# Attention values as 64 weight columns, and 16 convolution taps on TensorE, in a two-layer encoder kernel

## The chip, the cores and the metric

The kernel runs on one core of one Trainium2 chip. The metric is device time in microseconds (us): the median of three timed executions is 1800.13 us, the lowest 1799.9, the highest 1801.16. One more execution was recorded by the hardware profiler; all rows below come from it. TensorE is called PE (its weight loads PEld), VectorE DVE, ScalarE ACT, GpSimd POOL, SyncE SP.

## The reference, cut to what matters

Two layers work on x, 512 tokens by 1024 features, float32. Each is a feed-forward block, a mixing block and a second feed-forward block. The change lies in the mixing block alone:

```python
h = rms_norm(x, mix_norm);  p = h @ w_in
# group A: 8 heads, 96 columns for queries and keys, 64 for values, causal in chunks of 64 tokens
probs = softmax(scale * q @ k.T, masked);  attn = probs @ v          # per head, per 128 queries
# group B: 512 channels, causal depthwise convolution of 31 taps
u = a * sigmoid(g)
y[t, c] = conv_b[c] + sum over s in 0..30 of conv_w[30 - s, c] * u[t - s, c]
conv = silu(layer_norm(y, ln_g, ln_b))
x = x + concat(attn, conv) @ w_out
```

## The kernel before, in words

Activations are kept with features on the 128 partitions and the 512 tokens along the free axis. Products with large weights are made of three fp32r matmuls from operands split into a high and a low part (`mm3`, L153 to L157; its three matmuls have lines L154, L155, L156). Attention itself and the transposes are plain fp32 matmuls.

The mixing block is `mix_body` (L617). After the projections of w_in (`conv_in(c)` makes the four convolution groups u[0] to u[3] of 128 channels each, with `glu`), eight heads go through five stages, one step apart each by the table `ORDER = "t0s1p3v4o5"`: `turn` (L808) transposes queries and keys, `scores` (L821) makes scores, mask and exponentials, `turn_p` (L845) transposes the probabilities, `values` (L861) multiplies them with the values, `turn_out` (L879) transposes the result back to features on partitions, and `split` makes its high and low part, one entry of the list `at` for a pair of heads. In `values` the transposed probabilities are the stationary operand (128 columns) and 64 columns of values the moving one: ten matmuls per head, and DVE multiplies the pair's result by the reciprocals of the softmax sums (L875).

Beside the heads runs the convolution, one tap per instruction. The string `CONV = "DAAD"` gives the engine: groups 0 and 3 are accumulated by DVE in a PSUM bank (L922), groups 1 and 2 by ACT, which makes each product (L926), and POOL, which adds it (L930). POOL then sums the four groups (L944 to L946), a matmul with a constant matrix makes the mean over channels (L948), and the layer norm follows: DVE subtracts the mean (L954), squares are summed (L198), the reciprocal root is spread over the partitions (L217), DVE scales (L964), ACT applies silu (L966). Meanwhile PE makes the attention half of the first output products, the early groups (L936 to L940), until the normalised convolution arrives.

The order of instructions on each engine is fixed at build time by a scheduler that weighs estimated times; each engine takes its own list strictly in order. On SP stand the loads of weights; on POOL also the loads that accumulate low parts (L142).

## Time and profile before

| what | value |
|---|---|
| median of three executions | 1800.13 us (1799.9 to 1801.16) |
| the profiled execution, whole | 1798.87 us |
| its span, first to last instruction | 1797.1 us |
| granted PE clock, mean | 1.000 |
| PE busy | 1781.8 us (99%) |
| DVE busy | 1494.5 us (83%) |
| ACT busy | 1107.5 us (62%) |
| POOL busy | 421.5 us (23%) |

In a row of the timeline stand the start in us from the span's first instruction, the duration, engine, line, operation, result and operands, and in brackets how long the engine had been idle and what ended that. A matmul's duration reaches to the end of its way through the array, so that neighbours overlap: the distance from one start to the next is what it costs in a dense row. The profile shows one fp32 matmul as two records ("x2"). Rows of the chain of waits give the time that each piece holds the chain. In the table of windows each engine's busy time within a stretch stands beside the number of its instructions. The attention of the first layer runs from about 449.7 to 506 us, that of the second from 1339.7 to 1395.4 us, and the layer norm of the convolution right behind each.

### The profile page before, as it was taken

The numbers are of one execution on the slowest core, as the hardware profiler recorded it, in microseconds if no ns is written. First come the engines' busy times: TensorE is split into PE (matmuls) and PEld (weight loads), VectorE is DVE, ScalarE is ACT, GpSimd is POOL, SyncE is SP. The second block draws the span as 40 slices with busy tenths as digits, with TensorE's granted clock in tenths as the row PEclk, the third lists the DMA queues.
The fourth block names the chain that finished last, engine by engine and source line by source line (L and its number), as shares of the span: only waits on it lengthen the run. The fifth ranks groups of instructions, "written<-read, shape, count | busy, mean of one in ns | idle before, by whom it ended". The sixth has DMA issues, their size and how long they took to land.

```text
span 1797.1 us, 29235 instructions
## 1 busy us (share of the span) xinstructions
PE 1781.8 (99%) x11334; PEld 1602.4 (89%) x11334; DVE 1494.5 (83%) x2299; ACT 1107.5 (62%) x1721; POOL 421.5 (23%) x343
## 2 busy tenths in 40 slices
PE   9999999999999999999999999999999999999998
PEld 7899999888788899999888999998978788999997
DVE  7898988589956989898779989876998668989883
ACT  5575756457953575756645757554779435756564
POOL 1000000258943000000310000002689410000002
PEclk9999999999999999999999999999999999999999
DMA  5657575325103466665426575743250125575742
GB/s 168 171 131 182 135 177 123 109 88 134 33 22 102 123 164 161 155 160 132 123 65 170 122 194 122 193 112 111 81 147 7 46 82 160 140 183 134 182 117 74
DMA packets 70413, 226.16 MB, mean 126 GB/s; under 512 B 7937, under 2 KB 8321, under 8 KB 70273
## 3 DMA queue, kind: packets, MB, share of 16 engines
q1 hardware_dynamic: 54000, 169.74, 30.3%
q0 software_dynamic: 16128, 54.53, 18.0%
q8 instruction: 89, 1.46, 0.3%
q14 instruction: 52, 0.42, 0.1%
q10 hardware_dynamic: 144, 0.00, 0.0%
HBM read 222.15 MB, written 2.10 MB: 125 GB/s over the span
## 4 chain that ended last, share of the span: by engine, by line
PE 91%; ACT 3%; DVE 2%; POOL 2%; issue 1%; DMA 0%; SPq 0%; ACTq 0%; POOLq 0%; DVEq 0%
PE ps L154 24%; PE ps L156 23%; PE ps L155 23%; PE ps L373 11%; PE ps L374 6%; PE ps L868 1%; PE ps L834 1%; POOL y L930 1%; ACT pr L926 1%; ACT r L840 1%; PE ps L855 1%; PE ps L198 0%; POOL sck L173 0%; PE ps L217 0%; DVE wl L246 0%
## 5 line engine op out<-in xcount | busy, mean ns | idle before, releaser
L155 PE MATMUL ps<-r,wh 128*128 128x256 f32 (+1 forms) x2540 | 806.8, 318 | 0.0
L154 PE MATMUL ps<-r,wh 128*128 128x256 f32 (+1 forms) x2540 | 803.6, 320 | 2.2 <-ACT wh L138 0.7
L156 PE MATMUL ps<-r,wl 128*128 128x256 f32 (+1 forms) x2348 | 749.2, 321 | 0.0
L154 PEld LDWEIGHTS ps<-r,wh 128*128 128x128 f32 x2540 | 480.5, 189 | 47.0 <-ACT wh L138 3.6
L155 PEld LDWEIGHTS ps<-r,wh 128*128 128x128 f32 x2540 | 481.6, 190 | 35.8 <-DVE r L162 1.5
L156 PEld LDWEIGHTS ps<-r,wl 128*128 128x128 f32 x2348 | 445.1, 190 | 33.5 <-DVE wl L144 0.4
L373 PE MATMUL ps<-xj,wh 128*128 128x512 f32 x864 | 303.9, 392 | 0.0
L138 ACT CAST wh<-raw 128x1024 fp32r<-128x1024 f32 (+3 forms) x148 | 131.9, 899 | 208.1 <-PE ps L155 125.8
L390 POOL DMA_DIRECT2D ls<-in_wgu x72 | 62.7, 871 | 734.7 <-ACT ls L389 595.3
L244 ACT CAST wh<-fr 128x1024 fp32r<-128x1024 f32 (+1 forms) x160 | 157.6, 985 | 104.4 <-DVE fr L410 53.2
L144 DVE TENSOR_TENSOR wl<-raw,wh 128x1024 fp32r<-128x1024 f32 (+3 forms) x132 | 145.3, 1108 | 91.3 <-ACT wh L138 90.9
L246 DVE TENSOR_TENSOR wl<-fr,wh 128x1024 fp32r<-128x1024 f32 (+1 forms) x160 | 182.3, 1139 | 20.3 <-ACT wh L244 20.3
L373 PEld LDWEIGHTS ps<-xj,wh 128*128 128x128 f32 x864 | 161.4, 188 | 30.1
L930 POOL TENSOR_TENSOR y<-y,pr 128x511 f32<-128x511 f32 (+14 forms) x120 | 158.6, 1322 | 54.5 <-ACT pr L926 47.1
L374 PE MATMUL ps<-xj,ls 128*128 128x256 f32 x576 | 161.3, 280 | 0.0
L244 ACT CAST wh<-raw 128x1024 fp32r<-128x1024 f32 (+1 forms) x100 | 98.2, 982 | 45.1 <-PE ps L155 24.2
L246 DVE TENSOR_TENSOR wl<-raw,wh 128x1024 fp32r<-128x1024 f32 (+1 forms) x100 | 113.5, 1135 | 14.2 <-ACT wh L244 13.7
L191 POOL TENSOR_TENSOR r<-r,t 128x512 f32<-128x512 f32 x45 | 75.0, 1676 | 175.6 <-ACT t L187 174.8
L374 PEld LDWEIGHTS ps<-xj,ls 128*128 128x128 f32 x576 | 108.3, 188 | 0.0
L389 ACT ACTIVATE ls<-fr 128x1024 fp32r<-128x1024 f32 (+1 forms) x56 | 56.1, 1002 | 74.5 <-PE ps L374 42.8
L926 ACT ACTIVATE pr<-m,vec 128x511 f32<-128x511 f32 (+14 forms) x120 | 85.7, 736 | 13.2 <-POOL y L930 13.2
L922 DVE SCALAR_TENSOR_TENSOR cv<-m,vec,cv 128x511 f32<-128x511 f32 (+14 forms) x120 | 87.8, 732 | 3.6 <-ACT cv L918 2.2
(241 smaller groups left out, 2944.9 us busy)
## 6 DMA issues: line engine op xcount, KB each, us to landing
fr<-in_wgu SPq DMA_DIRECT2D x112, 512.0 KB, 4.2
ls<-in_wgu POOLq DMA_DIRECT2D x72, 512.0 KB, 6.2
raw<-in_wgu SPq DMA_DIRECT2D x62, 512.0 KB, 4.5
fr<-in_wdq SPq DMA_DIRECT2D x48, 384.0 KB, 4.6
ls<-in_wdq POOLq DMA_DIRECT2D x32, 384.0 KB, 4.8
raw<-in_wd SPq DMA_DIRECT2D x32, 384.0 KB, 3.2
raw<-in_wd SPq DMA_DIRECT2D x32, 256.0 KB, 2.8
raw<-in_wcv SPq DMA_DIRECT2D x16, 512.0 KB, 3.6
```

What stands on the lines that cost most here:

```text
L138: order["cast"] = A.copy(hi[:, :w], raw[:, :w]).ins
L144: (G if kind in POOLW.split() else V).tensor_tensor(lo[:, :w], raw[:, :w], hi[:, :w].bitcast(FP), ALU.subtract)
L154: T.matmul(o, lh, rh, start=first, stop=False, skip_group_check=free)
L155: T.matmul(o, lh, rl, start=False, stop=False, skip_group_check=free)
L156: order["mm"] = T.matmul(o, ll, rh, start=False, stop=last, skip_group_check=free).ins
L244: A.copy(hi[:, :w], src[:, :w])
L246: order["lo"] = V.tensor_tensor(lo[:, :w], src[:, :w], hi[:, :w].bitcast(FP), ALU.subtract).ins
L373: T.matmul(o, w[0][:, c], both, start=start and k == 0, stop=False, skip_group_check=True)
L374: last = T.matmul(o[:, 0:HS], w[1][:, c], both[:, 0:HS], start=False, stop=k == 3, skip_group_check=True).ins
L922: V.scalar_tensor_tensor(acc[:, s:], u[c][:, :S - s], tap(k), acc[:, s:], ALU.mult, ALU.add)
L926: A.activation(pr[:, s:], u[c][:, :S - s], AF.Copy, scale=tap(k))
L930: order["conv"] = G.tensor_tensor(acc[:, s:], acc[:, s:], pr[:, s:], ALU.add).ins
```

## The change

1. `values` works on a pair of heads. The values are now the stationary operand (64 columns) and the transposed probabilities the moving one (up to 512 columns); head one of the pair writes partitions 0 to 63 of the result, head two partitions 64 to 127. The result comes out with features on partitions, so `turn_out` has no transposes any more. The reciprocal sums are brought into that layout by eight small matmuls of a broadcast column with the identity (`pr`), copied by ACT, and multiplied in by DVE.
2. The first 16 taps of convolution group 2 are made on PE (`conv_pe`). Sixteen DMAs from SBUF to SBUF put four copies of 32 channels, shifted by 0 to 3 tokens, into each of four tiles; a matmul with a 128 by 32 matrix of tap weights then adds four taps for 32 channels, and four of these per 32 channels, shifted by 0, 4, 8, 12 tokens, make 16 taps. The 15 remaining taps of the group stay with ACT and POOL.
3. The last addition of the sum over groups moves from POOL to DVE. The accumulators of groups 1 and 2 get a buffer each under their own names (before: two buffers under one name), the products four buffers (before three).
4. One early group is placed ahead of the mean's matmul (`E1`), and the output products run in two rounds of four (before three, three, two).

```diff
-CONV = "DAAD"
+TAPS = (0, 31, 31, 0)
+Q = 32
+PT = 16
+PC = 2
+PSTEP = 3
-E1 = 0
-YP = 1
+E1 = 1
-WOG = 3
+WOG = 4
...
+        diag = kpool.tile([P, PT, Q], FP, tag="m", name=nm("m"), bufs=11)
+        G.tensor_tensor(diag, cst[:, None, CI32:CI32 + Q].to_broadcast([P, PT, Q]),
+                        vv(l, "cp")[:, :, None].to_broadcast([P, PT, Q]), ALU.mult)
+        shifted = []
...
-        ys = [None if kind == "D" else kpool.tile([P, S], FP, tag="y", name=nm("y"), bufs=2) for kind in CONV]
+        ys = [kpool.tile([P, S], FP, tag=f"y{c}", name=nm("y"), bufs=1) if n else None for c, n in enumerate(TAPS)]
...
             glu(*pp)
+            if c != PC:
+                return
+            for i in range(4):
+                v = slot()
+                V.memset(v[:, 0:4], 0.0)
+                for r in range(4):
+                    nc.sync.dma_start(out=v[r * Q:(r + 1) * Q, r:], in_=u[c][i * Q:(i + 1) * Q, 0:S - r])
+                shifted.append(v)
+
+        def conv_pe():
+
+            ps = bank()
+            for a in range(PT // 4):
+                for i in range(4):
+                    T.matmul(ps[i * Q:(i + 1) * Q, 4 * a:], diag[:, 4 * a + i], shifted[i][:, 0:S - 4 * a],
+                             start=a == 0, stop=a == PT // 4 - 1)
+            A.activation(ys[PC], ps, AF.Identity, bias=vv(l, "cb")[:, PC:PC + 1])
...
             if h % 2 == 0:
-                heads[h]["po"] = bank()
-            po = heads[h - h % 2]["po"].rearrange("p (t h d) -> p t h d", t=NT, h=2)
-            for t in range(NT):
-                for j in range(t + 1):
-                    T.matmul(po[:, t, h % 2], heads[h]["pt"][j][:, (t - j) * P:(t - j + 1) * P],
-                             vs[j][:, h * DV:(h + 1) * DV], start=j == 0, stop=j == t)
-            if h % 2 == 0:
                 return
             rs = small.tile([P, NT, 2], FP, tag="rs", name=nm("rs"))
             V.reciprocal(rs, heads[h - 1]["sums"])
+            pr = bank()
+            for t in range(NT):
+                for i in range(2):
+                    T.matmul(pr[i * DV:(i + 1) * DV, t * P:(t + 1) * P], rs[:, t, i:i + 1].to_broadcast([P, DV]),
+                             ident, start=True, stop=True)
+            r = tmp()
+            A.copy(r, pr)
+            po = bank()
+            for j in range(NT):
+                for i in range(2):
+                    T.matmul(po[i * DV:(i + 1) * DV, j * P:], vs[j][:, (h - 1 + i) * DV:(h + i) * DV],
+                             heads[h - 1 + i]["pt"][j], start=j == 0, stop=j == NT - 1)
             o = tmp()
-            V.tensor_tensor(o.rearrange("p (t h d) -> p t h d", t=NT, h=2), po,
-                            rs[:, :, :, None].to_broadcast([P, NT, 2, DV]), ALU.mult)
+            V.tensor_tensor(o, po, r, ALU.mult)
             heads[h]["o"] = o
...
-            ps = bank()
-            for t in range(NT):
-                T.transpose(ps[:, t * P:(t + 1) * P], o[:, t * P:(t + 1) * P], ident)
-            at.append(split(ps, kept if len(at) < 2 else slot))
+            at.append(split(heads[h]["o"], kept if len(at) < 1 else slot))
...
         for step in range(H + 6):
+            if step == PSTEP:
+                conv_pe()
...
-                pr = kpool.tile([P, S], FP, tag="pr", name=nm("pr"), bufs=3)
...
+            for s in range(PT if c == PC else 1, n):
+                k = CK - 1 - s
+                pr = kpool.tile([P, S], FP, tag="pr", name=nm("pr"), bufs=4)
+                A.activation(pr[:, s:], u[c][:, :S - s], AF.Copy, scale=tap(k))
...
-        (G if YP else V).tensor_tensor(ysum, ysum, ys[3], ALU.add)
+        V.tensor_tensor(ysum, ysum, ys[3], ALU.add)
```

The build places the sixteen matmuls of `conv_pe` on PE behind the last scores of head 1. In these rows ps is a PSUM bank, q and kn are queries and keys, m is a buffer (here the tap weights), r one of the shifted tiles or another ring buffer, cst the constants. Before, PE at this place:

```order
L834 MATMUL ps841_4817<-r817_4737,r815_4730 128x512
L835 LDWEIGHTS mrow_99
L835 MATMUL ps841_4817<-mneg_102,mrow_99 128x64
L811 MATMUL ps846_4838<-cst_74,q638_3853 96x128 x4
L816 MATMUL ps848_4845<-cst_74,kn639_3854 96x128 x4
L834 MATMUL ps850_4852<-r838_4813,r836_4806 128x128
```

And in the changed program (the row of 512 tokens stands four times, then four each of 508, 504 and 500):

```order
L859 MATMUL ps846_4843<-r822_4763,r820_4756 128x512
L860 LDWEIGHTS mrow_99
L860 MATMUL ps846_4843<-mneg_102,mrow_99 128x64
L664 MATMUL ps851_4864<-r795_4635,m631_3846 32x512
L664 MATMUL ps851_4864<-r796_4641,m631_3846 32x512
L664 MATMUL ps851_4864<-r797_4647,m631_3846 32x512
L664 MATMUL ps851_4864<-r798_4653,m631_3846 32x512
L664 MATMUL ps851_4864<-r795_4635,m631_3846 32x508
```

So the queries and keys of head 3 and the scores of head 2 now stand behind the convolution. The second place is the end of the attention. Before, PE there: the last values, the transposes of the last pair, the mean, the first early group.

```order
L868 MATMUL ps974_5294<-m824_4766,r973_5290 128x64
L868 MATMUL ps974_5294<-m826_4775,r971_5283 128x64
L886 MATMUL ps980_5328<-cst_74,t979_5326 128x128 x4
L948 MATMUL ps1058_5617<-t1057_5613,onesm_97 128x512
L154 MATMUL ps1060_5621<-m921_5105,wh984_5339 128x512
```

In the changed program the last pair begins with the eight broadcasts, six matmuls of the first early group stand inside its values,

```order
L895 MATMUL ps987_5331<-cst_74,rs986_5329 64x128 x8
L902 MATMUL ps989_5342<-r968_5264,m825_4774 64x512
L158 MATMUL ps1052_5587<-m927_5132,wh994_5359 128x512
L159 MATMUL ps1052_5587<-m928_5133,wh994_5359 128x512
L160 MATMUL ps1052_5587<-m927_5132,wl995_5361 128x512
L158 MATMUL ps1052_5587<-r965_5259,wh994_5359 128x512
L159 MATMUL ps1052_5587<-r966_5260,wh994_5359 128x512
L160 MATMUL ps1052_5587<-r965_5259,wl995_5361 128x512
L902 MATMUL ps989_5342<-r979_5307,m825_4774 64x512
L902 MATMUL ps989_5342<-r970_5271,m827_4783 64x384
```

and the rest of that group stands between the values and the mean (r991 and r992 are the high and low part of the last pair):

```order
L902 MATMUL ps989_5342<-r981_5314,m831_4801 64x128
L158 MATMUL ps1052_5587<-r984_5325,wh994_5359 128x512
L159 MATMUL ps1052_5587<-r985_5326,wh994_5359 128x512
L160 MATMUL ps1052_5587<-r984_5325,wl995_5361 128x512
L158 MATMUL ps1052_5587<-r991_5353,wh994_5359 128x512
L159 MATMUL ps1052_5587<-r992_5354,wh994_5359 128x512
L160 MATMUL ps1052_5587<-r991_5353,wl995_5361 128x512
L979 MATMUL ps1054_5604<-t1053_5600,onesm_97 128x512
```

In both programs four early groups stand ahead of the first product with the normalised convolution; before, all four behind the mean (L948), now one ahead of the mean (L979) and three behind. On DVE the end of the attention was, before (t is a temporary, y and m the accumulators):

```order
L162 TENSOR_TENSOR r977_5311<-ps975_5305,r976_5310 128x512
L875 TENSOR_TENSOR t979_5326<-ps974_5294,rs978_5324 128x512
L162 TENSOR_TENSOR r982_5334<-ps980_5328,r981_5333 128x512
L954 TENSOR_TENSOR m670_3986<-m670_3986,ps1058_5617 128x512
L954 TENSOR_TENSOR y631_3846<-y631_3846,ps1058_5617 128x512
```

and is now, with the last addition of the sum (L977) behind the low part of the last pair (L166):

```order
L905 TENSOR_TENSOR t990_5351<-ps989_5342,t988_5340 128x512
L166 TENSOR_TENSOR r992_5354<-t990_5351,r991_5353 128x512
L977 TENSOR_TENSOR t1053_5600<-t1053_5600,m810_4727 128x512
L985 TENSOR_TENSOR m671_3988<-m671_3988,ps1054_5604 128x512
L985 TENSOR_TENSOR y632_3848<-y632_3848,ps1054_5604 128x512
```

What moved there: the mean's matmul waits for L977, which stands behind L166 in DVE's list. On SP the sixteen copies (L656) stand behind the loads of the first four output weights and ahead of the next four.

40 lines of the change are left out of this document (22 added, 18 removed).

## The prediction

> **What bounds the kernel now.** I read the page's engine shares, then the table of windows for both mixing blocks, then PE's rows.
>
> ```profile
> PE 1781.8 (99%) x11334; PEld 1602.4 (89%) x11334; DVE 1494.5 (83%) x2299; ACT 1107.5 (62%) x1721; POOL 421.5 (23%) x343
> ```
> ```profile
> 449.70:465.00 15.30, 13.46 (x77) 8.60 (x75) 15.30 (x31) 15.30 (x38) 14.02 (x13) 1.00 0.41 87
> 465.00:506.00 41.00, 40.93 (x320) 35.80 (x320) 34.57 (x68) 35.48 (x86) 37.82 (x31) 1.00 0.01 2
> 506.00:521.40 15.40, 14.54 (x66) 10.99 (x64) 8.98 (x15) 6.37 (x11) 1.59 (x2) 1.00 0.00 0
> ...
> 1355.00:1395.40 40.40, 40.40 (x320) 35.51 (x318) 33.77 (x66) 35.50 (x85) 37.12 (x31) 1.00 0.01 1
> ```
> ```profile
> 449.70:494.60 44.90, 42.99 (x295) 33.16 (x294) 44.30 (x86) 43.85 (x107) 41.07 (x34) 1.00 0.14 31
> ```
>
> The columns are PE, PEld, DVE, ACT, POOL, then granted clock. PE is the bound of the whole kernel, and of the attention from 465 to 506: 40.93 of 41.00 us. But DVE, ACT and POOL are nearly full beside it: up to 494.6 DVE works 44.30 of 44.90 us. So time is saved only by taking work from PE without making another engine late, and any work added to PE is paid in full, twice, once per layer.
>
> The prices on PE come from the chain of waits, where each piece stands with the time that it holds PE:
>
> ```profile
> 466.23 1.12 PE ps L855 x10
> 467.35 2.28 PE ps L868 x20
> 469.63 0.49 PE ps L834 x2
> ...
> 471.43 0.22 PE ps L834 x2
> ...
> 471.69 0.73 PE ps L834 x2
> ...
> 472.45 0.94 PE ps L834 x2
> ...
> 503.51 0.44 PE ps L886 x4
> ...
> 508.43 0.23 PE ps L154
> ```
>
> L834's pieces are one fp32 matmul each with 256, 128, 384 and 512 moving columns: 0.49, 0.22, 0.73 and 0.94 us, in two passes ("x2"). The old values cost 2.28 us per head, a pair's transposes 0.44, an fp32r matmul of 512 columns 0.23.
>
> **The change part by part**, per layer.
>
> *Values.* Eight heads at 2.28 = 18.2 us go. New, a head streams 512, 384, 256 and 128 columns: 0.94 + 0.73 + 0.49 + 0.22 = 2.38 us, a pair 4.76, if PE does one pass at a time. The point of the new form is that two heads use different halves of the array's columns. No row of this trace shows passes of two such halves, so I bound it: all in sequence 4.76 us, all in pairs 2.38. I take two at a time: the two passes of one matmul need the same columns, so the second waits for the first, and in program order the other half's first pass can only join the second one. The first and last pass then stand alone: about 2.7 us a pair, 10.8 us a layer.
>
> *Broadcast of the reciprocals.* Eight matmuls of 128 columns at 0.22: 1.76 us in sequence, 0.9 in pairs; I take 1.0, so 4.0 a layer. Three transposes ahead of the last values go: 1.3 us (the fourth is in the tail below).
>
> *Convolution on PE.* Sixteen matmuls of about 512 columns: 14.8 us in sequence. With four quarters of the array all four could overlap, 3.9 us; by the same argument as for the values only two passes overlap: 7.6 us, which I take.
>
> *Change of shape.* In the program PE goes 16 times a layer between the full array and halves or quarters. No such change is in the trace. Where matmuls of unlike length follow each other:
>
> ```profile
> 513.84 0.95 PE L198 MATMUL ps<-ones,r 128*128 128x1 f32 x8
> 514.65 0.47 PE L154 MATMUL ps<-m,wh 128*128 128x512 f32 x1
> 514.97 0.39 PE L155 MATMUL ps<-m,wh 128*128 128x512 f32 x1
> ```
>
> the first long one holds PE 0.32 us (514.65 to 514.97), not 0.23: about 0.1 us is lost. The bounds are 0 and 0.16, the part of a matmul's 0.39 us that neighbours otherwise hide. I take 0.11, 1.8 us a layer. [...]
>
> *What fills waits.* PE waits for ACT's exponentials in the first part of the attention:
>
> ```profile
> 455.61 1.12 PE L834 MATMUL ps<-r,r 96*128 96x512 f32 x2 [0.42 <-ACT r L840]
> ...
> 462.62 0.64 PE L811 MATMUL ps<-cst,q 128*96 128x128 f32 x4 [0.33 <-ACT r L840]
> ...
> 465.07 1.12 PE L834 MATMUL ps<-r,r 96*128 96x512 f32 x2 [0.33 <-ACT r L840]
> ```
>
> The convolution is put behind the first of these; ACT catches up meanwhile, so the two later waits go: 0.7 us saved.
>
> *Relief of ACT and POOL.* Fifteen taps leave both, and one of the sum's additions leaves POOL:
>
> ```profile
> 471.15 31.48 POOL L930 TENSOR_TENSOR y<-y,pr 128x505 f32<-128x505 f32 x24 [0.39 <-ACT pr L926]
> 502.59 1.27 POOL L944 TENSOR_TENSOR t<-m,y 128x512 f32<-128x512 f32 x1
> ```
>
> ACT's products in layer zero (the table of windows for L926):
>
> ```profile
> 449.70:506.00 56.30, 26.57 (x37) 1.00 0.12 25
> ```
> ```profile
> 1397.33 1.13 PE L948 MATMUL ps<-t,onesm 128*128 128x512 f32 x2 [0.36 <-POOL t L946]
> ```
>
> POOL loses 15 x 31.48 / 24 = 20 us and ends long before PE; ACT loses 15 x 0.72 = 11 us and gets five evictions of about 0.6. I cost this at nothing, since PE's own list covers both; if PE had less to do, DVE would be next. POOL held the mean by 0.36 us in layer one alone, and that is in the tail below.
>
> *DMAs, DVE, POOL.* The sixteen copies wait for group 2's gate and stand in SP's queue:
>
> ```profile
> 437.38 0.69 DVE L632 TENSOR_TENSOR m<-t,t 128x512 f32<-128x512 f32 x1
> ```
> ```profile
> 440.00:445.00 5.00, 5.00 (x32) 4.37 (x31) 4.71 (x6) 3.59 (x5) 4.76 (x5) 1.00 0.99 224
> ```
> ```profile
> raw<-in_wout SPq DMA_DIRECT2D x7, 512.0 KB, 4.5
> ```
> ```profile
> DMA to landing us min/median/max: 5.6/6.7/9.0
> ```
> ```profile
> 530.16 2.00 ACT L138 CAST wh<-raw 128x1024 fp32r<-128x1024 f32 x2 [5.79 <-PE ps L155]
> ```
> ```profile
> POOL r L191 <- ACT t L187: 174.8, 17, 36.9
> ```
>
> They start at 438.1, when the DMA engines are full (0.99). Eight can be under way; each of the next eight waits for one of those, so there are two landings. A 512 KB load of the same queue lands in 4.5 us (the accumulating loads of POOL's queue, for which the third answer stands, in 5.6 to 9.0); at 4.5 each the copies are there by 448, and PE wants them at 456.6. Behind them on SP wait only loads of weights that ACT takes up at 530. I cost them at nothing; were they late, PE would stand, and with it scores, exponentials and DVE. The matrix of taps is made by POOL at the head of the block, where POOL waits for ACT anyway (last row: 174.8 us in 17 waits). Four small memsets on DVE: nothing.
>
> *The end of the attention.* Before, in both layers:
>
> ```profile
> 506.17 0.69 DVE L875 TENSOR_TENSOR t<-ps,rs 128x512 f32<-128x512 f32 x1 [0.87 <-PE ps L868]
> 508.22 0.69 DVE L162 TENSOR_TENSOR r<-ps,r 128x512 fp32r<-128x512 f32 x1 [1.37 <-ACT r L161]
> 508.83 0.68 DVE L954 TENSOR_TENSOR m<-m,ps 128x512 f32<-128x512 f32 x1
> ...
> 511.22 2.28 DVE L191 TENSOR_TENSOR r<-r,t 128x512 f32<-128x512 f32 x3
> ```
> ```profile
> 507.61 0.59 ACT L161 CAST r<-ps 128x512 fp32r<-128x512 f32 x1 [3.03 <-PE ps L886]
> ```
> ```profile
> 507.40 1.02 PE L948 MATMUL ps<-t,onesm 128*128 128x512 f32 x2
> ...
> 521.45 0.73 PE L154 MATMUL ps<-r,wh 128*128 128x512 f32 x2
> ```
> ```profile
> 1395.56 0.69 DVE L875 TENSOR_TENSOR t<-ps,rs 128x512 f32<-128x512 f32 x1 [0.87 <-PE ps L868]
> ```
> ```profile
> 1411.46 0.73 PE L154 MATMUL ps<-r,wh 128*128 128x512 f32 x2
> ```
>
> From the end of the values (506.12) to the first product with the convolution (521.45) it takes 15.3 us, in layer one 1395.51 to 1411.46, 15.95. Now the mean waits for the multiplication (0.69), ACT's high part (0.6), DVE's low part (0.69) and the sum's last addition (0.68), with hand-overs 2.9 us, where it was 1.3. From the mean to the convolution's first product it was 14.05 us; 0.3 of that was PE still busy with a second early group when the squares were ready (513.50, L198 at 513.84), and 0.4 DVE busy with L162, so 13.3 remain. Together 16.2: 0.9 us more in layer zero, 0.25 in layer one. That PE has one early group less behind the mean then costs nothing more, since it is done earlier: six of its matmuls ahead of the end of the values, 1.4 us.
>
> *Sum, up to the end of the values:* -18.2 - 1.3 + 10.8 + 4.0 + 7.6 + 1.8 - 0.7 + 1.4 = +5.4 us a layer. With the tail: 6.3 and 5.65, together 12 us. The profiled execution would go from 1798.87 to about 1811 us. The median of the runs shown stands 1.3 us above it: 1812.
>
> **The rivals.**
>
> *Full overlap, no loss at the change of shape (the other side).* Convolution 3.9, values 2.4 a pair, broadcasts 0.9: -18.2 - 1.3 + 9.6 + 3.6 + 3.9 - 0.7 + 1.4 = -1.7 a layer, with the tail -0.8 and -1.45. If in addition ACT's relief removes the first wait (0.42) and the six early matmuls fill a wait for the last evictions (1.4), -6 us in all: 1794. For it speaks that PE is full and ACT and POOL near it. Against it speaks DVE, whose taps are tied in its list to the scores of the last head:
>
> ```profile
> 493.98 0.71 DVE L922 SCALAR_TENSOR_TENSOR cv<-m,vec,cv 128x482 f32<-128x482 f32 x1
> ```
>
> DVE had 0.6 us to spare up to there, so the last tap cannot come earlier than about 493.4. Behind it PE still has three heads' transposes (3.4), one score (0.5), two broadcasts (1.8), two pairs of values (4.8) and the six early matmuls (1.4), 11.9 us: the values then end no earlier than 505.3, whatever PE saves. Then the result is 1798 to 1801, no measurable change. It decides at a convolution block under 4 us. [...]
>
> *No overlap.* Passes in sequence: 19.0 + 7.0 + 14.8 in place of 10.8 + 4.0 + 7.6 is 18.4 us more a layer: 1849. For it: every row shows fp32 passes one behind the other; against it: they all use the full array. It would show as 0.9 us between neighbouring matmuls of L664.
>
> *Shifted copies late.* With two landings of 9.0 us, the slowest of POOL's accumulating loads, and 2 us for the issues, they end at 458 to 460: PE stands some 3 us at L664 in each layer, 1818.
>
> **How the numbers follow.** My forecast with its own range (switches 0 to 0.3 us, convolution 6.5 to 7.7) runs from 1804 to 1820 and holds 0.5. Full overlap holds 0.28, of which 0.18 is below 1796.5 and 0.1 within 0.2%; no overlap 0.14; late copies 0.08. A measurement of this kernel tells 0.2%, 3.6 us, from no change. So faster 0.18, same 0.12 (a little from the forecast's lower end), slower 0.70. The range leaves out the sequence and the lowest part of full overlap: 1794 to 1838.
>
> **What would show it.** The distance between neighbours of L664 in PE's timeline: 0.47 us means two passes at a time, 0.24 four, 0.93 none. The eight broadcasts should take 1.0 us, a pair's values 2.7. The window of the attention should grow by 5 us with PE full, POOL near half busy and ACT some 6 us less busy; L979 should start 2.9 us after the last values, with PE idle for about 2 us between L979 and L158 of the convolution. I am wrong if a wait stands at L664, if PE is no longer full between 465 and the end of the values, or if neighbours of L664 are nearer than 0.4 us.

## The result, and the profile after

The changed kernel takes 1806.03 us (median of seven executions, 1803.89 to 1806.36) against 1799.04 us for the kernel before (seven, 1797.95 to 1801.16): a ratio of 1.0035, with a 95% interval of 1.0025 to 1.0044. It is slower by 7 us (0.35%), where 12 were forecast. Its span in the profile is 1804.5 us, 7.4 us more than the 1797.1 of before. In the code of after the lines of before have new numbers: L154 to L156 are L158 to L160, L161/L162 are L165/L166, L834 is L859, L855 is L880, L868 is L902, L875 is L905, L922 is L953, L926 is L957, L930 is L959, L944 to L946 are L975 to L977, L948 is L979, L191 is L195, L198 is L202, L217 is L221, L811, L816 and L840 (the transposes of queries and keys, ACT's exponentials) are L836, L841 and L865; L883 is DVE's copy of transposed probabilities. New are L664 (the convolution on PE) and L895 (the broadcasts).

The busy times of the page, and then the table of windows (PE, PEld, DVE, ACT, POOL, granted clock, DMA share, GB/s): attention and tail of layer zero, attention and tail of layer one. The tail runs from the end of the last values to the first product with the convolution. First after, then the same four stretches of before.

```profile
PE 1785.5 (99%) x11302; PEld 1584.6 (88%) x11302; DVE 1497.7 (83%) x2309; ACT 1095.8 (61%) x1699; POOL 382.7 (21%) x313
```
```profile
450.40:506.73 56.33, 55.92 (x392) 36.41 (x390) 48.72 (x95) 43.97 (x110) 31.30 (x26) 1.00 0.17 45
506.73:524.83 18.10, 15.02 (x54) 10.40 (x54) 9.71 (x16) 6.64 (x11) 1.03 (x1) 0.91 0.00 0
1343.70:1400.70 57.00, 56.12 (x392) 36.40 (x390) 49.17 (x95) 44.66 (x112) 31.70 (x27) 1.00 0.17 44
1400.70:1418.82 18.12, 15.04 (x55) 10.35 (x55) 9.72 (x16) 6.65 (x11) 1.03 (x1) 0.91 0.00 0
```
```profile
449.68:506.12 56.44, 54.53 (x397) 44.41 (x395) 49.89 (x97) 50.80 (x123) 51.98 (x43) 1.00 0.12 25
506.12:521.45 15.33, 14.42 (x66) 10.99 (x65) 9.03 (x15) 6.42 (x11) 1.47 (x2) 1.00 0.00 0
1339.70:1395.52 55.82, 54.37 (x397) 44.44 (x395) 48.96 (x95) 50.80 (x123) 51.30 (x43) 1.00 0.11 23
1395.52:1411.46 15.94, 14.68 (x65) 11.01 (x64) 9.11 (x15) 6.58 (x11) 2.71 (x3) 1.00 0.00 0
```

The attention is not longer: 56.33 against 56.44 us in layer zero, 57.00 against 55.82 in layer one. ACT has 6 to 7 and POOL 20 us less in it, about as forecast. The tail is 2.8 and 2.2 us longer, and in it PE is idle for 3 us and its granted clock is 0.91. The attention also starts 0.72 us late (450.40), and between the layers 0.6 us more go by. The sum: 0.72 - 0.11 + 2.77 + 0.62 + 1.18 + 2.18 = 7.4 us.

**The new work on PE** (rows of PE's timeline; the start of the next row says how long PE was held):

```profile
456.06 3.81 PE L664 MATMUL ps<-r,m 128*32 128x512 f32 x32
459.81 0.64 PE L836 MATMUL ps<-cst,q 128*96 128x128 f32 x4
...
463.19 1.29 PE L880 MATMUL ps<-cst,r 128*128 128x128 f32 x10
464.31 0.60 PE L836 MATMUL ps<-cst,q 128*96 128x128 f32 x4
...
473.21 1.29 PE L880 MATMUL ps<-cst,r 128*128 128x128 f32 x10
474.43 1.09 PE L895 MATMUL ps<-cst,rs 128*64 128x128 f32 x16
475.45 0.70 PE L859 MATMUL ps<-r,r 96*128 96x256 f32 x2
475.99 0.19 PE L860 MATMUL ps<-mneg,mrow 128*128 128x64 bf16 x1
476.29 2.37 PE L902 MATMUL ps<-r,m 128*64 128x512 f32 x16
478.60 0.64 PE L836 MATMUL ps<-cst,q 128*96 128x128 f32 x4
```

Sixteen matmuls of the convolution hold PE for 3.75 us, 0.234 us on average from one to the next, where the prediction had 14.8 us for one after the other: all four quarters of the columns work at once. In the trace's single records the first passes of three quarters start within 0.02 us of each other (456.07 to 456.09) and that of the fourth 0.25 us later; each second pass starts some 0.45 us behind its first. For the values the first passes of the two halves start 0.006 us apart. A pair's values take 2.31 us, where the prediction had 4.76 for two heads in sequence, and the eight broadcasts 1.02. A change of shape shows as 0.10 us each way: the ten transposes ahead of L895 hold PE 1.22 us, the ten ahead of L836 1.12; the broadcasts take 1.02 us where the full array follows, and 0.92 in the last two pairs, where the values follow at once. PE did not wait for the shifted copies, though the last of them was issued only at 451.5 and landed at 453.6, 2.5 us before PE wanted it (the forecast had them there by 448). In the trace the first eight of them signal on eight semaphores and the ninth, issued at 445.40, waits for the first one's; at most seven were under way at once, and one took 2.0 to 6.5 us to land (median 5.2).

**The tail**, on PE, layer zero:

```profile
501.81 1.02 PE L902 MATMUL ps<-r,m 128*64 128x512 f32 x2
502.76 0.51 PE L158 MATMUL ps<-m,wh 128*128 128x512 f32 x1
...
504.36 2.37 PE L902 MATMUL ps<-r,m 128*64 128x512 f32 x14
506.65 0.50 PE L158 MATMUL ps<-r,wh 128*128 128x512 f32 x1
...
508.23 0.50 PE L158 MATMUL ps<-r,wh 128*128 128x512 f32 x1 [0.61 <-ACT r L165]
508.95 0.50 PE L159 MATMUL ps<-r,wh 128*128 128x512 f32 x1 [0.22 <-DVE r L166]
...
509.64 1.10 PE L979 MATMUL ps<-t,onesm 128*128 128x512 f32 x2
...
515.60 1.29 PE L202 MATMUL ps<-ones,r 128*128 128x1 f32 x8 [2.10 <-DVE r L195]
516.75 0.77 PE L158 MATMUL ps<-m,wh 128*128 128x512 f32 x1
517.32 0.63 PE L159 MATMUL ps<-m,wh 128*128 128x512 f32 x1
...
520.91 1.02 PE L221 MATMUL ps<-t,ones 128*128 128x512 f32 x2
...
524.83 1.20 PE L158 MATMUL ps<-r,wh 128*128 128x512 f32 x4
```
```profile
513.00:515.00 2.00, 0.49 (x3) 0.07 (x1) 1.79 (x4) 0.98 (x2) 0.00 (x0) 1.00 0.00 0
515.00:517.00 2.00, 1.40 (x9) 1.43 (x10) 0.53 (x2) 0.00 (x0) 0.00 (x0) 0.80 0.00 0
517.00:519.00 2.00, 2.00 (x5) 1.55 (x6) 0.78 (x2) 0.00 (x0) 1.03 (x1) 0.50 0.00 0
519.00:521.00 2.00, 2.00 (x9) 1.63 (x8) 0.00 (x0) 0.00 (x0) 0.00 (x0) 0.85 0.00 0
```

Three things are to be seen. First, six matmuls of the early group (502.76 to 504.36, 1.60 us) stand between the first matmul of the last pair's values and the rest. That first matmul now has no partner on the other half and holds PE 0.95 us alone; in two pieces the values take 0.95 + 2.29 = 3.24 us instead of 2.3. The six between them hold PE 0.2 us more than 6 x 0.23, two changes of shape. Second, the mean (509.64) comes 2.91 us behind the end of the values, as forecast. Third, PE idles for 2.10 us ahead of the row sums (L202), and behind that its granted clock is 0.50: matmuls of 512 columns follow each other at 0.43 us instead of 0.23, so that L221 comes 5.31 us after the row sums, where it came 3.68 us after them before (513.84 for the row sums in the prediction's rows, and this row of before):

```profile
517.52 1.02 PE L217 MATMUL ps<-t,ones 128*128 128x512 f32 x2
```

### The profile page after: what moved, and what is told of

It is laid out like the page before. It is cut to its first block, busy times and chain, and to the rows that moved or that the text cites. A ratio compares the mean times of both kernels' runs of the same rounds, so it can differ in the third digit from the quotient of the medians.

```text
span 1804.5 us, 29201 instructions
## 1 busy us (share of the span) xinstructions
PE 1785.5 (99%) x11302; PEld 1584.6 (88%) x11302; DVE 1497.7 (83%) x2309; ACT 1095.8 (61%) x1699; POOL 382.7 (21%) x313
## 4 chain that ended last, share of the span: by engine, by line
PE 56%; DVE 3%; ACT 1%; POOL 0%; issue 0%; ACTq 0%; DVEq 0%; POOLq 0%
PE ps L158 14%; PE ps L160 14%; PE ps L159 14%; PE ps L377 7%; PE ps L378 4%; DVE cv L953 1%; PE ps L902 0%; PE ps L859 0%; DVE mx L861 0%; DVE wl L250 0%; PE ps L202 0%; POOL sck L177 0%; PE ps L880 0%; PE ps L221 0%; DVE kn L810 0%
## 5 line engine op out<-in xcount | busy, mean ns | idle before, releaser
L158 PE MATMUL ps<-r,wh 128*128 128x256 f32 (+1 forms) x2556 | 810.7, 321 | 4.1 <-ACT r L165 1.4
L160 PE MATMUL ps<-r,wl 128*128 128x256 f32 (+1 forms) x2364 | 756.3, 322 | 0.2 <-DVE wl L250 0.2
L158 PEld LDWEIGHTS ps<-r,wh 128*128 128x128 f32 x2556 | 484.1, 189 | 50.5 <-ACT wh L142 3.6
L160 PEld LDWEIGHTS ps<-r,wl 128*128 128x128 f32 x2364 | 448.6, 190 | 34.8 <-DVE wl L148 0.7
L959 POOL TENSOR_TENSOR y<-y,pr 128x495 f32<-128x495 f32 (+29 forms) x90 | 120.8, 1343 | 46.6 <-ACT pr L957 41.0
L195 POOL TENSOR_TENSOR r<-r,t 128x512 f32<-128x512 f32 x45 | 74.1, 1656 | 128.8 <-ACT t L191 128.2
L953 DVE SCALAR_TENSOR_TENSOR cv<-m,vec,cv 128x511 f32<-128x511 f32 (+14 forms) x120 | 87.8, 732 | 3.7 <-ACT cv L949 2.2
L394 POOL DMA_DIRECT2D ls<-in_wdq x32 | 27.7, 865 | 262.2 <-ACT ls L393 262.2
```

The source lines that it names most:

```text
L158: T.matmul(o, lh, rh, start=first, stop=False, skip_group_check=free)
L160: order["mm"] = T.matmul(o, ll, rh, start=False, stop=last, skip_group_check=free).ins
L394: G.dma_start(out=lo[:, :n], in_=w, accum_op=ALU.add)
L953: V.scalar_tensor_tensor(acc[:, s:], u[c][:, :S - s], tap(k), acc[:, s:], ALU.mult, ALU.add)
L959: order["conv"] = G.tensor_tensor(ys[c][:, s:], ys[c][:, s:], pr[:, s:], ALU.add).ins
```

## The experiments

Theory A: the attention is as long as before because the overlap is complete, and the loss lies in the tail, in the place of the early group, in the addition on DVE and in the clock behind the idle. Theory B, called rival B in the expectations: the attention is longer by the work added to PE, and the early group only moves matmuls. The table gives what PE's rows show of each run (layer zero / layer one): from the first score to the end of the values, from there to the mean, from the mean to the row sums, and from those to L221.

| kernel | median, us | attention | to the mean | to the row sums | to L221 |
|---|---|---|---|---|---|
| before | 1799.04 | 56.44 / 55.82 | 1.28 / 1.81 | 6.44 / 6.53 | 3.68 / 3.68 |
| after | 1806.03 | 56.33 / 57.00 | 2.91 / 2.92 | 5.96 / 5.96 | 5.31 / 5.31 |
| tail_both | 1793.97 | 53.74 / 54.41 | 0 / 0 | 6.99 / 6.99 | 3.75 / 3.75 |
| tail_no_early | 1802.44 | 53.75 / 54.41 | 2.93 / 2.94 | 9.34 / 8.04 | 3.67 / 3.67 |
| tail_pool_add | 1805.33 | 56.34 / 56.96 | 2.80 / 2.80 | 5.88 / 5.88 | 5.32 / 5.32 |
| tail_fill | 1803.06 | 56.35 / 56.96 | 2.92 / 2.91 | 5.95 / 5.96 | 3.75 / 3.73 |
| values_alone | 1805.89 | 53.60 / 54.26 | 3.95 / 3.96 | 8.82 / 9.40 | 3.67 / 3.67 |
| conv_alone | 1803.77 | 57.85 / 58.47 | 1.28 / 1.28 | 6.43 / 6.43 | 3.67 / 3.68 |
| conv_in_turn | 1803.76 | 58.58 / 59.21 | 0 / 0 | 6.99 / 6.99 | 3.73 / 3.75 |
| half_conv | 1792.47 | 52.89 / 53.50 | 0 / 0 | 6.98 / 6.99 | 3.75 / 3.73 |

### The tail: four kernels

tail_both: both edits in the tail undone.

```diff
-E1 = 1
+E1 = 0
...
-        V.tensor_tensor(ysum, ysum, ys[3], ALU.add)
+        G.tensor_tensor(ysum, ysum, ys[3], ALU.add)
```

> The changed kernel with no early group ahead of the mean and the sum's last addition on POOL again. Theory A (the attention is no longer than before, the loss is in the tail): the values end 1.4 us earlier, the mean stands 0.2 us behind them instead of 3.0, TensorE does not idle behind it, its granted clock stays 1.00, and from the mean to the convolution's first product it takes 14.05 us as in the kernel before instead of 15.2. Together some 5.3 us a layer: about 1794 us against 1804.5, 0.3% under the kernel before. Rival B (the attention is longer because of the convolution and the broadcasts, and the early group only moves matmuls): 1803 to 1806.

Measured: 1793.97 us (1793.17 to 1794.87), ratio to the kernel before 0.9967, interval 0.9955 to 0.998: 12 us below after and faster than both. PE's rows:

```profile
501.50 2.32 PE L902 MATMUL ps<-r,m 128*64 128x512 f32 x16
503.75 1.13 PE L979 MATMUL ps<-t,onesm 128*128 128x512 f32 x2
...
510.74 1.02 PE L202 MATMUL ps<-ones,r 128*128 128x1 f32 x8 [0.35 <-DVE r L195]
...
514.49 1.02 PE L221 MATMUL ps<-t,ones 128*128 128x512 f32 x2
...
518.41 1.20 PE L158 MATMUL ps<-r,wh 128*128 128x512 f32 x4
```

The values stand in one piece again (2.25 us), the attention is 2.6 us shorter in each layer, the mean follows at once, and there is no half clock. Theory A had 1.4 us for the early group; it cost 2.6, and that is why the span fell by 13.1 us and not by 10.5.

tail_no_early: only the early group.

```diff
-E1 = 1
+E1 = 0
```

> The changed kernel with no early group ahead of the mean; the last addition stays on DVE behind the last pair. Theory A: the values end 1.4 us earlier, the mean still 2.9 us behind them, now with TensorE idle there. If an idle of that length halves the granted clock afterwards, the two groups behind the mean take 7.1 us instead of 5.5 and the gain is 1.5 us a layer, 1801.5 us; if it does not, 3 us a layer, 1798.5 us. Rival B: 1803 to 1806.

Measured: 1802.44 us (1799.51 to 1804.7), ratio 1.0015 (1.0006 to 1.0024).

```profile
507.45 2.04 PE L979 MATMUL ps<-t,onesm 128*128 128x512 f32 x2 [2.93 <-DVE t L977]
508.51 1.42 PE L158 MATMUL ps<-m,wh 128*128 128x512 f32 x1
509.72 0.63 PE L159 MATMUL ps<-m,wh 128*128 128x512 f32 x1
```

The idle of 2.93 us is now ahead of the mean, and the half clock follows it there: the mean holds PE 1.06 us, where in after it was 0.54, and the two groups behind it end so late that the row sums stand 9.34 us behind the mean. In layer one they stand 8.04 us behind it: the clock is 0.50 for 6.83 us in layer zero and for 3.41 in layer one. Without that they would stand 6.99 us behind it, as in tail_both. A good part of the 2.6 us that the attention gains is lost again. Of the two cases in the expectation the one with the half clock came true.

tail_pool_add: only the addition.

```diff
-        V.tensor_tensor(ysum, ysum, ys[3], ALU.add)
+        G.tensor_tensor(ysum, ysum, ys[3], ALU.add)
```

> The changed kernel with the sum's last addition on POOL alone; the early group stays ahead of the mean. Theory A: POOL has the sum ready by 502 us, but the mean stands on TensorE behind three matmuls that wait for the last pair's low part, so it comes only 0.1 to 0.2 us earlier, and the idle of 2.1 us behind it stays: 1804 us, no change that can be told. A rival in which DVE's addition itself is the cost of the tail: the mean 0.7 us earlier in each layer, 1803 us or less.

Measured: 1805.33 us (1803.64 to 1807.12), ratio 1.0029 (1.0017 to 1.004): no change that can be told, the mean 0.1 us earlier. It still stands on PE behind three matmuls that wait for the last pair's low part. So two paths end within 0.1 us of each other ahead of the mean, the early group and the addition. The addition on DVE costs nothing that can be told beside the early group; it costs 2.9 us as soon as that group is no longer in the way. The two edits have to be undone together.

tail_fill: nine matmuls more behind the mean, into a bank that is not read.

```diff
+        with tc.issue_after(heads[H - 1][EARLY]):
+            again = bank()
+            for k in range(3):
+                c = slice(k * P, (k + 1) * P)
+                mm3(again, wo[1][0][:, c], wo[1][1][:, c], *at[k], k == 0, k == 2)
         early_groups(range(E1, E2))
```

> The changed kernel with nine more matmuls (three quarters of an output group computed once more into a bank that nobody reads, 2.04 us) where TensorE idles for 2.1 us behind the mean. If the idle is what halves the granted clock in the 3 us behind it, the clock stays 1.00, the row sums start as late as now, and from them to L221 it takes 3.7 us instead of 5.3: 1.6 us a layer, about 1801.3 us in spite of more work. If the clock falls for another reason (the narrow matmuls of the row sums), 1804 to 1806.

Measured: 1803.06 us (1802.08 to 1805.01), 3 us below after with 4 us more work on PE; span 1801.3.

```profile
513.00:515.00 2.00, 2.00 (x10) 1.64 (x9) 1.90 (x4) 1.57 (x3) 0.00 (x0) 1.00 0.00 0
515.00:517.00 2.00, 1.98 (x14) 1.46 (x12) 0.94 (x2) 0.00 (x0) 0.00 (x0) 1.00 0.00 0
517.00:519.00 2.00, 2.00 (x10) 1.66 (x11) 0.61 (x2) 0.00 (x0) 1.03 (x1) 1.00 0.00 0
```

PE does not idle there, the clock stays at 1.00 with the same row sums, and L221 comes 3.75 us after them. So the idle is what lowers the clock here (0.50 behind 2.10 us in after, 1.00 without it), and the lower clock costs 1.6 us a layer (5.31 against 3.75) beside the idle itself.

### The two parts alone

Both start from tail_both, so that the tail does not disturb. values_alone leaves `conv_pe` with its copies and its matrix away, and the sixteen taps go back to ACT and POOL.

```diff
-PC = 2
+PC = 9
...
-            if step == PSTEP:
-                conv_pe()
```

> The run with the tail undone (no early group ahead of the mean, the last addition on POOL; 1794 us, attention 53.7 and 54.4 us from the first score to the end of the values), and in it no convolution on TensorE: the sixteen taps go back to ACT and POOL. TensorE has 3.75 us and two changes of shape less. If TensorE alone holds the attention, it falls by 3.5 to 4 us, to 50 us; if DVE's list holds it as well (42.56 of the 43.32 us up to its last tap, untouched here), by 0.7 us at the most, to 53. In both cases POOL has its 20 us back and ends its sum at about 506 as in the kernel before, so the mean waits for it and the time is about 1797 to 1799 us, no better than before.

Measured: 1805.89 us (1804.91 to 1806.43), ratio 1.0037 (1.0025 to 1.005), where 1797 to 1799 was expected. POOL ended its sum late, as said, and the mean (L974 in this kernel) waited:

```profile
508.00 2.07 PE L974 MATMUL ps<-t,onesm 128*128 128x512 f32 x2 [3.95 <-POOL t L972]
```

The wait was forecast (POOL at 506; it became 508); what it does to the clock was not: behind the idle of 3.95 us the row sums come 8.82 us after the mean instead of 6.99. The attention takes 53.60 us, hardly less than with the convolution (53.74), though PE has nearly 4 us less to do. The reason stands in PE's rows: it waits eight times for ACT's exponentials (L862 here, L865 in after), 2.74 us in sum in layer zero, where tail_both has no such wait; three of the largest:

```profile
458.43 0.91 PE L856 MATMUL ps<-r,r 96*128 96x384 f32 x2 [0.42 <-ACT r L862]
...
472.80 1.09 PE L892 MATMUL ps<-cst,rs 128*64 128x128 f32 x16 [0.44 <-ACT r L862]
...
482.59 0.64 PE L838 MATMUL ps<-cst,kn 128*96 128x128 f32 x4 [0.43 <-ACT r L862]
```

So the two parts belong together. The new values give PE time of which it can use little as long as ACT has all its products, and the sum is ready in time only if POOL has fewer additions; the convolution on PE relieves both, for 0.14 us of attention.

conv_alone keeps the convolution on PE and takes `values` and `turn_out` from the kernel before.

```diff
...
-                    T.matmul(po[i * DV:(i + 1) * DV, j * P:], vs[j][:, (h - 1 + i) * DV:(h + i) * DV],
-                             heads[h - 1 + i]["pt"][j], start=j == 0, stop=j == NT - 1)
+                    T.matmul(po[:, t, h % 2], heads[h]["pt"][j][:, (t - j) * P:(t - j + 1) * P],
+                             vs[j][:, h * DV:(h + 1) * DV], start=j == 0, stop=j == t)
...
```

> The same run with the old values and their transposes, and the convolution on TensorE. TensorE has 3.75 us and two changes of shape (0.2 us) more than the kernel before, ACT and POOL have the relief. If TensorE holds the attention: 3.2 to 4 us more a layer (0.7 us of waits for ACT filled), 59.5 us, and 1805 to 1807 us. If the attention of before was held by DVE, ACT or POOL and not by TensorE: 0 to 1 us more, 1799 to 1801.

Measured: 1803.77 us (1802.81 to 1804.65), ratio 1.0027 (1.0017 to 1.0037), between the two expectations. The attention is 1.41 and 2.65 us longer than before, of 3.95 us added: more of PE's waits are filled than the 0.7 us of the forecast. In the attention of before PE waits 1.81 and 1.34 us for ACT's exponentials (the waits of 0.15 us or more in its rows), in conv_alone not at all in layer zero and 0.42 us in layer one.

### The order of the sixteen matmuls

conv_in_turn, from tail_both: the loops over shifts and quarters change places, so that neighbours want the same quarter.

```diff
-            for a in range(PT // 4):
-                for i in range(4):
+            for i in range(4):
+                for a in range(PT // 4):
```

> The same run (tail undone), with the sixteen matmuls of the convolution in another order: the four that add to one quarter of the columns follow each other, so that neighbours want the same quarter. If overlap comes from neighbours that use different quarters: 0.93 us from one to the next, 14.8 us for the block instead of 3.75, 11 us more on TensorE a layer, of which 10 to 11 arrive if TensorE has no slack: 1814 to 1816 us. If the order does not matter: 3.75 us and 1794.

Measured: 1803.76 us (1803.48 to 1804.4), ratio 1.0024 (1.0014 to 1.0034).

```profile
456.15 8.80 PE L664 MATMUL ps<-r,m 128*32 128x512 f32 x32
```

The block takes 8.80 us, neither 3.75 nor 14.8. Order matters, but later quarters still begin beside earlier ones: in the trace's records the four quarters begin at 456.15, 457.89, 459.63 and 461.37, each 1.74 us behind the one before, while the eight passes of a quarter take 0.43 us each, 3.4 us in all. So two quarters work at a time. Of the 5.0 us added, 4.8 us arrive in the attention of each layer (58.58 and 59.21 against 53.74 and 54.41): beside the new values PE has next to no slack for more work.

### What holds the attention now

The rival of full overlap in the prediction said that DVE's taps would hold the attention. less_dve, again from tail_both, gives DVE fewer taps: PE takes them from the fourth group instead of the third, and seven of the third go to DVE. It also has three buffers for ACT's products instead of four.

```diff
-TAPS = (0, 31, 31, 0)
+TAPS = (0, 31, 24, 16)
-PC = 2
-PSTEP = 3
+PC = 3
+PSTEP = 5
...
-                pr = kpool.tile([P, S], FP, tag="pr", name=nm("pr"), bufs=4)
+                pr = kpool.tile([P, S], FP, tag="pr", name=nm("pr"), bufs=3)
```

> The same run (tail undone), with the sixteen taps on TensorE taken from the fourth group, which DVE computes, instead of the third; seven taps of the third go from ACT and POOL to DVE. The convolution stands two steps later. DVE has 4 to 5 us a layer less, POOL 11 us more than in the run with the tail undone, and still 9 less than in the kernel before. If DVE holds the attention beside TensorE, it gets 1 to 2 us shorter and the time is 1790 to 1792 us; if TensorE alone holds it, 53.5 to 54.4 us as now and 1793 to 1795 us.

Measured: 1816.66 us (1816.25 to 1820.24), ratio 1.0102 (1.0089 to 1.0116). The kernel missed its aim: DVE's taps moved to the end of its list, the last addition of a DVE accumulator came at 510.9, and POOL waited for it 12.48 us and the mean for POOL 9.45 us. The attention itself takes 54.15 and 54.85 us, 0.4 us more than in tail_both, though DVE had waits of up to 4.8 us in it; with four things changed at once this says little on DVE.

The next kernels leave work out, from tail_both: six DVE taps of the first group (six_taps_less), half of the convolution on PE (half_conv), both (both_less).

```diff
-            for s in range(n, CK):
+            for s in range(n, CK if c else CK - 6):
...
-            for a in range(PT // 4):
+            for a in range(PT // 8):
```

> The run with the tail undone, without the last six of the 31 taps of the first group, which DVE computes in 0.71 us each (left out; nothing takes their place): 4.3 us less on DVE a layer, the other engines unchanged. The attention there takes 53.74 and 54.41 us. If DVE's list holds it, it gets 2 to 4 us shorter in each layer and the time falls to 1787 to 1790 us; if TensorE holds it, less than 0.5 us and 1793 to 1794; if both do, with some tenths of a microsecond between them, the same.

> The run with the tail undone, with only the first eight of the sixteen matmuls of the convolution (the other eight taps left out): 1.9 us less on TensorE a layer. If TensorE alone holds the attention, it gets 1.7 to 1.9 us shorter in each layer, 1790 us; if DVE's list holds it, 0 to 0.4 us, 1793 to 1794; if both do, the same 0 to 0.4.

> Both taken away, six taps on DVE and half of the convolution on TensorE. If TensorE alone holds the attention: as with half of the convolution, 1790 us. If DVE alone: as with six taps less. If both hold it, neither of the two single runs gets more than some tenths, and this one 1.5 to 1.9 us in each layer: 1790 to 1791 us.

Measured: 1797.61 (1794.71 to 1800.77), 1792.47 (1791.2 to 1793.23) and 1796.55 us (1794.83 to 1798.6). The first and the third settle nothing on the attention. The taps of the first group lie ahead of it in DVE's list (30 taps stand in it with and without them); it began 1.7 and 2.1 us later in layer zero (451.80 and 452.17) and 3.2 us later in layer one, and took 53.23 / 53.22 and 53.05 / 53.74 us, up to 1.2 us less than in tail_both. What shortened it is not shown, and the ten executions of the first lie 6 us apart. half_conv shortened it by 0.85 and 0.91 us, half of the 1.9 us taken away; waits, of which tail_both has none in layer zero, fill the rest:

```profile
464.92 0.64 PE L841 MATMUL ps<-cst,kn 128*96 128x128 f32 x4 [0.27 <-DVE r L883]
469.01 0.64 PE L836 MATMUL ps<-cst,q 128*96 128x128 f32 x4 [0.34 <-ACT r L865]
469.95 0.70 PE L859 MATMUL ps<-r,r 96*128 96x256 f32 x2 [0.30 <-ACT r L865]
474.45 1.09 PE L895 MATMUL ps<-cst,rs 128*64 128x128 f32 x16 [0.21 <-ACT r L865]
```

So four more kernels took the work from inside the attention: six taps of the fourth group from DVE, seven products of the third from ACT and POOL, and both with half of the convolution.

```diff
-            for s in range(n, CK):
+            for s in range(n, CK - 6 if c == 3 else CK):
...
-            for s in range(PT if c == PC else 1, n):
+            for s in range(PT if c == PC else 1, n - 7 if c == PC else n):
```

> The run with the tail undone, without the last six of the 31 taps of the fourth group (left out), which DVE computes among the heads: 4.2 us less on DVE in each attention. The attention takes 53.74 and 54.41 us there, and 52.89 and 53.50 with half of the convolution left out on TensorE. If DVE alone holds it, it falls by 2 to 4 us a layer; if TensorE, DVE and ACT are within a few tenths of each other, by 0.3 to 0.9 us.

> The same run, without the last seven taps of the third group (left out), which ACT multiplies and POOL adds: 5 us less on ACT and 9 us less on POOL in each attention. If ACT alone holds it (it is full from 452 to 480 us), the attention falls by 2 to 4 us a layer; if the three engines are within a few tenths of each other, by 0 to 0.9 us.

> Six taps of the fourth group and half of the convolution on TensorE left out. If DVE and TensorE hold the attention between them, 1.5 to 2 us less a layer; if ACT holds it with them, no more than 0.9 us, as with half of the convolution alone.

> All three left out: six taps on DVE, half of the convolution on TensorE, seven products on ACT and POOL. If the three engines are in balance, only now the attention falls by 1.7 us or more a layer, to 52 us or less; if something else holds it, it stays at 53.

| kernel | median, us | ratio to before, interval | attention |
|---|---|---|---|
| tail_both | 1793.97 | 0.9967 (0.9955 to 0.998) | 53.74 / 54.41 |
| dve_less | 1794.95 | 0.9977 (0.9967 to 0.9986) | 53.98 / 54.63 |
| act_less | 1794.39 | 0.9969 (0.9959 to 0.998) | 53.83 / 54.44 |
| half_conv | 1792.47 | 0.996 (0.9946 to 0.9975) | 52.89 / 53.50 |
| dve_pe_less | 1793.17 | 0.9965 (0.9952 to 0.9978) | 52.86 / 53.51 |
| all_less | 1791.48 | 0.9958 (0.9944 to 0.9973) | 52.74 / 53.37 |

4.2 us less on DVE, or 5 us less on ACT, bring nothing; half of the convolution brings 0.9 us alone, 0.9 with DVE's taps left out as well, and 1.0 with ACT's too. So the attention did not show the balance of two or three engines that the first cases of the last two expectations had; their second cases came true in the number, but the cause that one of them names, ACT, is not shown by it. What the runs show is that PE's work sets the length of the attention as it stands: 5.0 us more of it arrive to 4.8 us (conv_in_turn), 1.9 us less to 0.9 (half_conv). DVE is busy for 48.7 of 53.7 us beside it in tail_both, and yet the end of its list decides nothing. What gives half of PE's relief back are the waits between 464 and 475 us; the work left out on DVE and ACT comes last in their lists and was no relief there, so which of the two holds PE in that stretch is open.

## Why the prediction was wrong in its size, and where it was right

Right were the sign (0.70 for slower) and the range (1794 to 1838), the 2.9 us from the values to the mean, the idle of about 2 us behind it, the price of a change of shape (0.11 forecast, 0.10 measured), the relief of ACT and POOL, and that the shifted copies are hidden. The 2 us that the rival of late copies gives to their issues was an estimate that no run shows: SP took 15.02 us for the sixteen in after (437.07 to 452.09).

The sign was luck as far as the mechanism goes. Of the 12 us that were forecast, 10.8 were to come from PE's work in the attention and 1.15 from the tail. Of the 7.4 us measured, 1.07 came from the attention, 4.95 from the tail and 1.34 from stretches that no step had; with the tail undone the same work on PE is 0.3% faster than before (tail_both). Its terms, us per layer:

| term | forecast | measured |
|---|---|---|
| old values and three transposes removed | -19.5 | 17.7 and 1.35 in PE's rows of before, -19.0 |
| new values | +10.8 | 4 x 2.3 = 9.2 |
| broadcasts | +4.0 | 2 x 1.02 + 2 x 0.92 = 3.9 |
| convolution on PE | +7.6 | 3.75 |
| sixteen changes of shape | +1.8 | 14 x 0.10 = 1.4, in part within the rows above; two more in the early matmuls |
| waits filled | -0.7 | -1.81 / -0.92 (1.81 / 1.34 before, 0 / 0.42 after) |
| six early matmuls | +1.4 | 2.6 |
| to the end of the values | +5.4 | -0.11 / +1.18 |
| tail | +0.9 / +0.25 | +2.77 / +2.18 |

**The step that failed** is "I take two at a time: the two passes of one matmul need the same columns, so the second waits for the first, and in program order the other half's first pass can only join the second one". The second pass does wait for the first: in after it starts some 0.45 us behind it in the convolution. But the other part's first pass does not wait for the first part's second: it starts beside the first pass (0.006 us apart in the values). For the values that was nearly harmless (2.3 instead of 2.7). For the convolution it doubled the price, 7.6 us for 3.75: four quarters in turn do overlap four times. That passes start strictly in program order no row of before shows; it was the author's estimate. In the trace of after most neighbours among three of the quarters start 6 to 7 ns apart, and conv_in_turn does not show that order: the second quarter's first matmul starts at 457.89, ahead of the first quarter's last passes at 458.73 and 459.15, so that for PE's passes there the "strictly in order" in the description of the kernel before does not hold. By strict order only the last pass of one quarter could join the first of the next, an estimate of some 12.3 us (29 passes in turn at 0.43); it took 8.80.

**The second term** is the six early matmuls, 1.4 us for 2.6. They were costed as work alone, but they stand inside the last pair's values and part two heads that run together: 1.6 us with two changes of shape, and 0.95 for a matmul that has lost its partner, so that 3.24 + 1.60 us stand where tail_both has 2.25.

**The third** is the step "so 13.3 remain" from the mean to the convolution's first product. It was 15.2: the idle of 2.1 us was foreseen, but costed as if PE went on at full clock behind it. The row sums to L221 took 5.31 us instead of 3.68.

The measured terms add up to 0.0 and +0.9 us to the end of the values, where the windows show -0.11 and +1.18; closer than some 0.5 us the sum is not to be trusted, because the rows contain a part of the changes. Against the windows the forecast has 5.51 and 4.22 us too much; in the tail it has 1.87 and 1.93 too little, and 1.34 us go by ahead of the two attentions, which no step had: 12.0 - 9.73 + 3.80 + 1.34 = 7.4 us. The prediction had named its own mark, neighbours of L664 nearer than 0.4 us; they stand 0.234 apart on average.

The rival of full overlap had the overlap right and yet ended at 1794 to 1801. It lacked the changes of shape, the price of parting the values, and the tail with its clock, and its floor at 505.3 us from DVE's last tap is no floor: dve_less takes six taps away, and the attention gets no shorter.

What is left open: why the attention starts 0.72 us later in layer zero. In all the runs it starts between 449.4 and 452.9 us. Some small operations of DVE are stretched there, beside POOL's additions and DMA issues; in after these two (POOL's additions of L959 start at 438.16 and 439.97, its issues of L146 at 437.50 and 439.36), whose shortest take 0.42 and 0.21 us:

```profile
437.66 2.35 DVE L810 TENSOR_TENSOR kn<-cke,scp 128x256 f32<-128x256 f32 x1
439.93 1.95 DVE L807 TENSOR_SCALAR scp<-sck,ratio 128x8 f32<-128x8 f32 x1
```

Before has two such operations there as well (1.67 and 1.86 us); that they cause the later start is not shown.

## What to carry to other kernels

Work packed into columns of the array was cheap here while neighbours in program order used different columns (0.234 us from one matmul to the next on four quarters, 0.55 in conv_in_turn); what was put between the partners, though useful work, cost its own time and that of the partner left alone (1.60 and 0.95 us in after). Before an idle of PE is costed, ask what its clock does behind it: here 2.1 us without a matmul cost another 1.6. A forecast that is right in sign can be wrong in every large term: check where the time went, stage by stage. Two edits that look independent can hide each other: of the early group and the addition on DVE either could be undone for 0.7 to 3.6 us, both together for 12.

## What the runs showed of the hardware that was not expected

The granted clock falls to 0.50 after an idle of 2.08 to 2.11 us (both layers of after and of tail_pool_add). It does not fall where nine matmuls fill the gap (tail_fill), nor in before after this shorter one:

```profile
506.91 0.66 PE L886 MATMUL ps<-cst,t 128*128 128x128 f32 x4 [0.78 <-DVE t L875]
```

In before the clock is 1.00 throughout the tail (the table of windows above). The trace of after has the fall at 516.20, 0.6 us after the idle has ended, and the rise at 519.61: 3.41 us. In tail_no_early the fall comes 2.2 us into the idle of layer zero and the half clock lasts 6.83 us; in layer one the fall comes 1.2 us after an idle of the same 2.93 us, and the half clock lasts 3.41. After the idle of 9.45 us in less_dve it lasts 10.24. These are one, two and three times 3.41 us, and the two falls of after lie 894.29 us apart, 262 such steps. In every fall of these tails the 3.41 us ahead of it hold 2.07 us of idle or more. The same idle of 2.93 us costs 2.35 us behind it in layer zero of tail_no_early and 1.05 in layer one (9.34 and 8.04 us to the row sums, where it is 6.99 in tail_both). That the difference comes from where the idle lies against these steps is the author's estimate from these figures; whether 2.1 us that lie across two of them cost anything is not shown. Of the seven executions of after three took 1803.9 to 1804.7 us and four 1806.0 to 1806.4; one slow stretch fewer would make such a step, but that this is its cause is not shown.

Sixteen fp32 matmuls on four quarters of the columns take 3.75 us, and the eight on two halves that make a pair's values 2.31. A pass of 512 columns takes 0.43 us there, less than the 0.47 that the prediction read from the scores' rows; at that price the passes in sequence would take 13.6 and 4.3 us. The overlap is worth a factor of 3.6 and 1.9. What is missing from 4 and 2 is mostly the 0.25 us by which the fourth quarter starts late, and the 0.10 us at a change of shape.
